# Token mixing of a two-layer trunk: rotation, key stacks, probabilities and values divided anew among VectorE, ScalarE, GpSimd and DMA

## The chip, the cores and the metric

The kernel runs on one core of a Trainium2 chip. The metric is the device time of one execution in microseconds (us). The page and the trace name the engines PE (TensorE's matmuls), PEld (its weight loads), DVE (VectorE), ACT (ScalarE), POOL (GpSimd) and SP (SyncE, which issues the weight loads from HBM). ACTq is ScalarE's queue: DMAs that ScalarE issues are shown there.

## The reference

The reference is a decoder trunk in float32: 256 tokens, width 1024, two layers. Each layer is a half-weighted SwiGLU block, a mixing of tokens, and a second SwiGLU block; a final norm follows. The change lies in the mixing:

```
h = rms_norm(x);  proj = h @ w_in
q, k       = partial rotation of the first 16 of 64 columns of a head:
             (x1*cos - x2*sin, x2*cos + x1*sin, rest)
NSA:  8 query heads, 2 key/value groups; compressed, selected and
      window attention, each times a sigmoid gate, added up
MoBA: 8 heads, causal attention within one block of 256
softmax:  p = exp(s - max) / max(sum, 1);  out = p @ v
x = x + concat(o_nsa, o_moba) @ w_out
```

With 256 tokens all four selected blocks are visible, and the window is wider than the sequence, so the selected and the window attention share scores of plain causal form, one set for each of two key projections.

## The kernel before

The activations are held transposed (features on partitions, tokens along the row). A float32 product is made of three passes in the fp32r format: high part times high part, high times low, low times high. So every weight block of 128x1024 is loaded by SP ("wraw"), cast by ScalarE (line 254, "whi") and subtracted by VectorE (line 283, "wlo"); the class `Stream` hands the blocks to TensorE in the order in which they are used. `pump` and `split` start the splits of blocks to come, as far as the seven slots allow. A scheduler orders each engine's instructions at build time from the order in the source and its own model of durations; at run time each engine's queue is strictly in order.

`mixer` (from line 747) is the mixing of one layer. `feature_one` makes 128 feature rows of a projection in a PSUM bank (four banks "psA", two "psB", one "psC", one "psD"). The rotation of two such sets of rows (128x512 values) is split in two. `rope_begin` (line 759) copies the bank to SBUF ("raw", line 762), has ScalarE issue two DMAs that swap the row pairs to be rotated into SW (lines 763 and 764), and multiplies the bank by the cosine table (line 765, VectorE). `rope_end` (line 767), called later, multiplies SW by the sine table and adds it (lines 768 and 769, both GpSimd). There are seven rotations a layer: query rows 0 and 1, the keys KK, query rows 2 and 3, and four of the MoBA part (`m_feat`, line 1058: keys mk and queries mq, two each; `m_end` ends one).

`stack_q` (line 773) writes a query's high and low part on the two halves of the partitions. `stack_k` (line 798) casts the rotated keys to a high part (line 802, ScalarE) and a low part (line 803, VectorE) on one half of the partitions of KK; `repeat_k` (line 805) copies them to the other half by two DMAs on ScalarE's queue (line 807). `m_stack` and `m_repeat` (lines 1078 to 1093) do the same for the MoBA keys KM.

Scores go to psB and psC (`nsa_s`, line 1026; `moba_s`, line 1188). `softmax` (line 976) masks, scales and takes the maximum on VectorE (lines 984 and 985), then ScalarE exponentiates with a sum (lines 988 and 989). `normalize` (line 992) takes the reciprocals on VectorE and multiplies the probabilities P on GpSimd (lines 1000 and 1001): a 128x256 and a 128x128 part for each of two branches of the eight NSA heads and once for each of the eight MoBA heads. `transpose_p` turns P on TensorE (line 1008) and ScalarE copies it out (line 1010); `pv` multiplies with the values, which ScalarE read from psA with the norm's factor: VN for NSA (line 1122) and MV for MoBA (line 1112, after a `pump` of `m_v`). The output product (`out_block`, lines 539 to 541) takes up the banks of psA afterwards.

Of the kernel before, what the change touches and what calls it, by code (L numbers as in the profile page):

```python
# [21 lines left out]
F32 = mybir.dt.float32  # L22
# [111 lines left out]
def constants():  # L134
# [6 lines left out]
    for h in range(2):  # L141
        for d in range(half):
            C[h * 64 + 8 * d] = C[h * 64 + 8 * d + 4] = cos[:, d]
            Sg[h * 64 + 8 * d] = -sin[:, d]
            Sg[h * 64 + 8 * d + 4] = sin[:, d]
# [165 lines left out]
def trunk(ctx, tc, xin, wst, w1st, gains, glast, cst, small, out, phases=PHASES, n_raw=5, n_hl=7):  # L311
# [435 lines left out]
    def mixer(pi, l):  # L747
# [11 lines left out]
        def rope_begin(b, raw, sw, ro, ctab):  # L759

            src = b.rearrange("p (a t) -> p a t", a=2)
            A.copy(raw, src)
            A.dma_start(sw[0:128:8], raw[4:128:8])
            A.dma_start(sw[4:128:8], raw[0:128:8])
            V.tensor_mul(ro, src, ctab[:, None, :].to_broadcast([128, 2, S]))

        def rope_end(sw, ro, stab):
            G.tensor_mul(sw, sw, stab[:, None, :].to_broadcast([128, 2, S]))
            G.tensor_add(ro, ro, sw)
# [28 lines left out]
        def stack_k():  # L798

            for g in range(2):  # L800
                src = rotk[half[g]].rearrange("p a (b t) -> p b a t", b=2)
                A.copy(KK[g][half[g], 0], src)
                V.tensor_sub(KK[g][half[g], 1], src, KK[g][half[g], 0].bitcast(F32))

        def repeat_k():
            for g in range(2):
                A.dma_start(KK[g][half[1 - g]].bitcast(F32), KK[g][half[g]].bitcast(F32))
# [33 lines left out]
        rotk = rawk[:, 2:4]  # L841
# [5 lines left out]
        rope_begin(b1, rawq[:, 0:2], SW[:, 0:2], rotq[:, 0:2], con("C"))  # L847
# [21 lines left out]
        rope_begin(b2, rawk[:, 0:2], SW[:, 2:4], rotk, CK)  # L869
# [3 lines left out]
        rope_end(SW[:, 0:2], rotq[:, 0:2], con("Sg"))  # L873
# [4 lines left out]
        rope_begin(b3, rawq[:, 2:4], SW[:, 0:2], rotq[:, 2:4], con("C"))  # L878
        rope_end(SW[:, 2:4], rotk, SK)
# [3 lines left out]
        rope_end(SW[:, 0:2], rotq[:, 2:4], con("Sg"))  # L883
        repeat_k()
# [107 lines left out]
        def normalize(key):  # L992
# [6 lines left out]
            for r in range(nb):  # L999
                G.tensor_mul(P[:, 0:2, r], P[:, 0:2, r], sm[:, 0, r:r + 1, None].to_broadcast([128, 2, 128]))  # L1000
                G.tensor_mul(P[:, 2, r], P[:, 2, r], sm[:, 1, r:r + 1].to_broadcast([128, 128]))
# [54 lines left out]
        cur, ends, stacks, reps = {}, [], [], []  # L1056

        def m_feat(which, i):
# [5 lines left out]
            if i % 2 == 1:  # L1064
                h = i // 2
                raw = mp.tile([128, 2, S], F32, name="mraw", tag="F", bufs=2)
                tabs = (CK, SK) if which == "mk" else (con("C"), con("Sg"))
                sw, ro = SW[:, 2 * h:2 * h + 2], cur["rot"][:, 2 * h:2 * h + 2]
                rope_begin(cur["b"], raw, sw, ro, tabs[0])
# [264 lines left out]
```

## Time and profile before

| | us |
|---|---|
| median of 3 runs | 1040.21 |
| lowest, highest run | 1039.88, 1041.37 |
| the profiled execution | 1037.38 |
| its span, first to last instruction | 1035.6 |
| busy: PE, DVE, ACT, POOL | 1000.6, 688.5, 593.3, 326.1 |

The profiled execution is another one than the three timed runs. Its rows are exact for itself alone; a difference of two kernels is read from the timed runs. Busy time of PE counts matmuls that overlap each other, so its share says where PE had nothing under way, not how near it is to its peak. The granted clock of the execution was 0.999 of full speed. The first layer's mixing lies at about 199 to 342 us of the span, the second layer's at about 707 to 851 us.

### The profile page before, as it was taken

Reading aid. Unit: us, or ns where it says so; the run is one execution under the profiler, and the core shown is the slowest. Engines: PE = TensorE matmul, PEld = TensorE weight load, DVE = VectorE, ACT = ScalarE, POOL = GpSimd, SP = SyncE. Lnnn points to the kernel's source line nnn. Section 1 sums busy time; section 2 is a strip of 40 time slices with the busy share of each in tenths; the row PEclk is TensorE's granted clock in tenths of the full one; section 3 lists DMA queues with packets and bytes.
Section 4 is the critical chain, followed back from the end, with each engine's and each line's share of the span. In section 5 each row is a group of like instructions: output and inputs, shape, how many; then the busy total and the mean of one; then the engine's idle time right before and its main releaser. Section 6 shows DMA issues by size and latency. Waiting matters only on the chain.

```text
span 1035.6 us, 16186 instructions
## 1 busy us (share of the span) xinstructions
PE 1000.6 (97%) x5861; PEld 861.0 (83%) x5861; DVE 688.5 (66%) x1187; ACT 593.3 (57%) x1137; POOL 326.1 (31%) x425
## 2 busy tenths in 40 slices
PE   9999999998998999999999999999999989999997
PEld 7788888898776888888888888889888778888885
DVE  6766666589865766566676666566986648666664
ACT  6745555457766655555565555545677747555552
POOL 3622232145641422222232223121475313222230
PEclk9999999999999999999999999999999999999999
DMA  8685776455444466666556677764543426666531
GB/s 268 241 279 186 274 240 218 145 171 157 114 126 125 154 198 196 188 197 186 163 182 203 186 234 239 262 196 138 181 131 108 143 82 208 194 209 193 193 122 41
DMA packets 52848, 188.21 MB, mean 182 GB/s; under 512 B 6368, under 2 KB 6496, under 8 KB 51616
## 3 DMA queue, kind: packets, MB, share of 16 engines
q1 hardware_dynamic: 49680, 182.04, 55.4%
q10 hardware_dynamic: 3088, 5.14, 2.0%
q8 instruction: 46, 0.75, 0.3%
q14 instruction: 34, 0.28, 0.1%
HBM read 182.04 MB, written 1.05 MB: 177 GB/s over the span
## 4 chain that ended last, share of the span: by engine, by line
PE 83%; DVE 7%; ACT 5%; issue 2%; DMA 2%; POOL 1%; ACTq 0%; POOLq 0%; DVEq 0%
PE psB L560 15%; PE psA L539 9%; PE psA L540 9%; PE psA L541 9%; PE psB L562 8%; PE psD L560 8%; PE psC L560 7%; PE psD L562 4%; PE psC L562 4%; DVE wlo L283 3%; PE psA L533 2%; PE psA L532 2%; PE psA L534 2%; ACT whi L254 1%; PE psA L398 1%
## 5 line engine op out<-in xcount | busy, mean ns | idle before, releaser
L283 DVE TENSOR_TENSOR wlo<-wraw,whi 128x1024 fp32r<-128x1024 f32 x325 | 408.2, 1259 | 242.1 <-ACT whi L254 240.5
L254 ACT CAST whi<-wraw 128x1024 fp32r<-128x1024 f32 (+1 forms) x326 | 339.5, 1044 | 304.2 <-issue 175.4
L560 PE MATMUL psB<-x,whi 128*128 128x512 f32 x688 | 243.1, 394 | 3.4 <-DVE hs L627 3.3
L635 POOL TENSOR_TENSOR hs<-hs,rbc 128x256 f32<-128x256 f32 x88 | 75.0, 853 | 380.3 <-DVE hs L627 364.6
L562 PE MATMUL psB<-x,wlo 128*128 128x256 f32 x688 | 192.5, 280 | 0.0
L560 PEld LDWEIGHTS psB<-x,whi 128*128 128x128 f32 x688 | 129.2, 188 | 32.5 <-DVE hs L627 4.3
L541 PE MATMUL psA<-wlo,hp 128*128 128x512 f32 x352 | 136.9, 389 | 0.0
L540 PE MATMUL psA<-whi,hp 128*128 128x512 f32 x352 | 136.8, 389 | 0.0
L539 PE MATMUL psA<-whi,hp 128*128 128x512 f32 x352 | 136.2, 390 | 0.0
L562 PEld LDWEIGHTS psB<-x,wlo 128*128 128x128 f32 x688 | 129.4, 188 | 1.4
L637 POOL TENSOR_TENSOR hs<-hs,rbc 128x256 f32<-128x256 f32 x88 | 102.9, 1170 | 80.5 <-ACT hs L636 80.5
L560 PE MATMUL psC<-x,whi 128*128 128x512 f32 x352 | 124.9, 392 | 0.0
L560 PE MATMUL psD<-x,whi 128*128 128x512 f32 x352 | 124.8, 392 | 0.0
L562 PE MATMUL psC<-x,wlo 128*128 128x256 f32 x352 | 98.6, 280 | 0.9 <-DVE wlo L283 0.9
L562 PE MATMUL psD<-x,wlo 128*128 128x256 f32 x352 | 98.4, 280 | 0.0
L560 PEld LDWEIGHTS psC<-x,whi 128*128 128x128 f32 x352 | 66.1, 188 | 14.5
L560 PEld LDWEIGHTS psD<-x,whi 128*128 128x128 f32 x352 | 66.1, 188 | 14.4
L541 PEld LDWEIGHTS psA<-wlo,hp 128*128 128x128 f32 x352 | 66.1, 188 | 13.9
L539 PEld LDWEIGHTS psA<-whi,hp 128*128 128x128 f32 x352 | 66.0, 188 | 13.7
L540 PEld LDWEIGHTS psA<-whi,hp 128*128 128x128 f32 x352 | 66.1, 188 | 12.3
L532 PE MATMUL psA<-x,whi 128*128 128x256 f32 x256 | 72.8, 284 | 1.2 <-ACT PT L1010 0.8
L533 PE MATMUL psA<-x,whi 128*128 128x256 f32 x256 | 72.3, 283 | 0.7 <-DVE x L380 0.7
(229 smaller groups left out, 1586.3 us busy)
## 6 DMA issues: line engine op xcount, KB each, us to landing
wraw<-in_w SPq DMA_DIRECT2D x318, 512.0 KB, 4.3
W1a<-in_w SPq DMA_DIRECT2D x4, 1024.0 KB, 6.3
W1mixn<-in_w SPq DMA_DIRECT2D x2, 1024.0 KB, 7.6
W1late<-in_w SPq DMA_DIRECT2D x2, 1024.0 KB, 6.5
KM<-KM ACTq DMA_DIRECT2D x8, 256.0 KB, 3.2
wraw<-in_w SPq DMA_DIRECT2D x4, 420.0 KB, 3.7
wraw<-in_w SPq DMA_DIRECT2D x4, 256.0 KB, 5.1
X<-in_small SPq DMA_DIRECT2D x1, 1024.0 KB, 9.5
```

The source lines that it names most:

```text
L254: self.last_hi = self.nc.scalar.copy(hi[:, a:b], raw[:, a:b]).ins
L283: eng.tensor_sub(lo[:, :c], raw[:, :c], hi[:, :c].bitcast(F32))
L532: T.matmul(o, hi, xh, start=first, stop=False, skip_group_check=True)
L533: T.matmul(o, hi, xl, start=False, stop=False, skip_group_check=True)
L534: T.matmul(o, lo, xh, start=False, stop=last, skip_group_check=True)
L539: T.matmul(o, parts[:, 0, c], hi, start=first, stop=False, skip_group_check=True)
L540: T.matmul(o, parts[:, 1, c], hi, start=False, stop=False, skip_group_check=True)
L541: T.matmul(o, parts[:, 0, c], lo, start=False, stop=last, skip_group_check=True)
L560: T.matmul(o, blk128(hi, k), x.rearrange("p a t -> p (a t)"), start=k == 0, stop=k == KT - 1, skip_group_check=True)
L562: T.matmul(o[:, S:], blk128(lo, k), x[:, 0], start=False, stop=k == KT - 1, skip_group_check=True)
L635: G.tensor_mul(g, g, state["rbc"])
L637: G.tensor_mul(g, g, state["rbc5"])
```

## The change

Four parts of the mixing are rewritten, and nothing outside it but the sign of a table.

- Rotation: VectorE multiplies the bank by the sine table (with opposite sign) first, the DMAs swap rows of that product into SW, VectorE multiplies the bank by the cosine table, and `rope_end` is one add on VectorE. The raw copy by ScalarE is made only for the two query sets that the compressed scores read.
- Key stacks: ScalarE and VectorE write both halves of the partitions of KK and KM themselves; `repeat_k` and `m_repeat` with their six DMAs a layer are gone.
- Probabilities: the multiplication by the reciprocal sums is a `tensor_scalar` on VectorE in place of a product on GpSimd.
- Values: of VN and of MV, ScalarE reads the first block of tokens and VectorE the second; MV is read ahead of the `pump` in `m_v(3)` and not after it.

```diff
-            Sg[h * 64 + 8 * d] = -sin[:, d]
-            Sg[h * 64 + 8 * d + 4] = sin[:, d]
+            Sg[h * 64 + 8 * d] = sin[:, d]
+            Sg[h * 64 + 8 * d + 4] = -sin[:, d]
...
-        def rope_begin(b, raw, sw, ro, ctab):
+        def rope_begin(b, raw, other, sw, ro, tabs):
             src = b.rearrange("p (a t) -> p a t", a=2)
-            A.copy(raw, src)
-            A.dma_start(sw[0:128:8], raw[4:128:8])
-            A.dma_start(sw[4:128:8], raw[0:128:8])
-            V.tensor_mul(ro, src, ctab[:, None, :].to_broadcast([128, 2, S]))
-
-        def rope_end(sw, ro, stab):
-            G.tensor_mul(sw, sw, stab[:, None, :].to_broadcast([128, 2, S]))
-            G.tensor_add(ro, ro, sw)
+            ctab, stab = (t[:, None, :].to_broadcast([128, 2, S]) for t in tabs)
+            V.tensor_mul(other, src, stab)
+            A.dma_start(sw[0:128:8], other[4:128:8])
+            A.dma_start(sw[4:128:8], other[0:128:8])
+            V.tensor_mul(ro, src, ctab)
+            if raw is not None:
+                A.copy(raw, src)
+
+        def rope_end(sw, ro):
+            V.tensor_add(ro, ro, sw)
...
-                A.copy(KK[g][half[g], 0], src)
-                V.tensor_sub(KK[g][half[g], 1], src, KK[g][half[g], 0].bitcast(F32))
-
-        def repeat_k():
-            for g in range(2):
-                A.dma_start(KK[g][half[1 - g]].bitcast(F32), KK[g][half[g]].bitcast(F32))
+                own = KK[g][half[g], 0]
+                for r in (half[g], half[1 - g]):
+                    A.copy(KK[g][r, 0], src)
+                for r in (half[g], half[1 - g]):
+                    V.tensor_sub(KK[g][r, 1], src, own.bitcast(F32))
...
-                G.tensor_mul(P[:, 0:2, r], P[:, 0:2, r], sm[:, 0, r:r + 1, None].to_broadcast([128, 2, 128]))
-                G.tensor_mul(P[:, 2, r], P[:, 2, r], sm[:, 1, r:r + 1].to_broadcast([128, 128]))
+                V.tensor_scalar(P[:, 0:2, r], P[:, 0:2, r], sm[:, 0, r:r + 1], None, op0=OP.mult)
+                V.tensor_scalar(P[:, 2, r], P[:, 2, r], sm[:, 1, r:r + 1], None, op0=OP.mult)
...
-                A.copy(K[half[a], :, a, 0], ro[half[a]])
-                V.tensor_sub(K[half[a], :, a, 1], ro[half[a]], K[half[a], :, a, 0].bitcast(F32))
-            reps.append(K)
-
-        def m_repeat():
-            K = reps.pop(0)
-            for a in range(2):
-                A.dma_start(K[half[1 - a], :, a].bitcast(F32), K[half[a], :, a].bitcast(F32))
+                own = K[half[a], :, a, 0]
+                for r in (half[a], half[1 - a]):
+                    A.copy(K[r, :, a, 0], ro[half[a]])
+                for r in (half[a], half[1 - a]):
+                    V.tensor_sub(K[r, :, a, 1], ro[half[a]], own.bitcast(F32))
...
             st.done(u[0])
+            if i == 3:
+                A.activation(MV[:, 0], cur["vb"][0], AF.Copy, scale=rs[:, 0:1])
+                V.tensor_scalar(MV[:, 1], cur["vb"][1], rs[:, 1:2], None, op0=OP.mult)
             st.pump()
-            if i == 3:
-                for blk in range(2):
-                    A.activation(MV[:, blk], cur["vb"][blk], AF.Copy, scale=rs[:, blk:blk + 1])
...
-        for blk in range(2):
-            A.activation(VN[:, blk], vb[blk][:, :S], AF.Copy, scale=rs[:, blk:blk + 1])
+        A.activation(VN[:, 0], vb[0][:, :S], AF.Copy, scale=rs[:, 0:1])
+        V.tensor_scalar(VN[:, 1], vb[1][:, :S], rs[:, 1:2], None, op0=OP.mult)
```

The callers of `rope_begin` and `rope_end` pass both tables, a scratch tile "other" (or, in `m_feat`, a new tile "rots" in place of "mraw"), and no raw tile where none is needed. The calls of `repeat_k` and `m_repeat` are taken out; all other calls keep their order.

## Rows read from the trace of the kernel before

**Rows 1.** The page, part 1: busy us, share of the span, instructions.

```profile
PE 1000.6 (97%) x5861; PEld 861.0 (83%) x5861; DVE 688.5 (66%) x1187; ACT 593.3 (57%) x1137; POOL 326.1 (31%) x425
```

**Rows 2.** Layer 0 in stretches: length, busy (count) of PE, PEld, DVE, ACT, POOL.

```profile
213.00:236.60 23.60, 22.11 (x216) 20.15 (x215) 22.21 (x26) 13.28 (x21) 11.73 (x8) 1.00 0.63 193
236.60:291.00 54.40, 51.41 (x375) 45.17 (x376) 43.04 (x133) 39.16 (x114) 38.34 (x54) 1.00 0.48 138
291.00:332.00 41.00, 36.49 (x206) 27.73 (x205) 25.56 (x71) 26.93 (x65) 9.70 (x14) 1.00 0.42 128
```

**Rows 3.** The waits of PE, 232 to 300 us: total us, times, longest us.

```profile
PE psA L539 <- ACT late L1112: 1.8, 1, 1.8
PE psB L1031 <- DVE qs L778: 1.5, 1, 1.5
PE psD L1048 <- ACT PcT L969: 1.0, 1, 1.0
PE psB L1031 <- DVE mx L984: 1.0, 1, 1.0
...
PE psB L1031 <- DMA KK<-KK: 0.3, 1, 0.3
```

**Rows 4.** The waits of PE, 740 to 810 us (layer 1).

```profile
PE psA L539 <- ACT late L1112: 1.6, 1, 1.6
PE psB L1031 <- DVE qs L778: 1.3, 1, 1.3
```

**Rows 5.** Timeline of ACT's queue: start us, us, what.

```profile
231.18 2.19 ACTq L807 DMA_DIRECT2D KK<-KK  x2
```

**Rows 6.** DMA issues: queue, count, KB each, median us to landing.

```profile
KK<-KK ACTq DMA_DIRECT2D x4, 256.0 KB, 5.3
...
SW<-mraw ACTq DMA_DIRECT2D x16, 32.0 KB, 2.0
```

**Rows 7.** DVE's groups of the whole run: busy us, mean ns, idle before.

```profile
L456 DVE TENSOR_TENSOR yg<-X,gain 128x512 f32<-128x512 f32 x4 | 2.8, 691 | 0.1
...
L465 DVE TENSOR_SCALAR yg<-yg,ny 128x512 f32<-128x512 f32 x2 | 1.0, 486 | 0.1
...
L528 DVE TENSOR_SCALAR gain<-gain 128x1024 f32<-128x1024 f32 x1 | 0.7, 694 | 2.1 <-DMA gain<-in_glast 2.1
```

**Rows 8.** Timeline of DVE: start us, us, instruction, [idle before].

```profile
238.42 1.23 DVE L283 TENSOR_TENSOR wlo<-wraw,whi 128x1024 fp32r<-128x1024 f32 x1 [1.38 <-ACT whi L254]
239.56 0.18 DVE L1119 TENSOR_SCALAR GT<-GT 128x48 f32<-128x48 f32 x1
...
240.15 0.39 DVE L984 CUSTOM_DVE_ANT_0 P<-psB,const,rs 128x256 f32<-128x256 f32 x1
```

**Rows 9.** Line 1001 on POOL: duration ns min/median/max.

```profile
L1001 POOL TENSOR_TENSOR P<-P,sm x48: 389/400/1382, 246.6 to 831.6; 128x128 f32<-128x128 f32 x48
```

**Rows 10.** DVE's groups, 236.6 to 291 us.

```profile
L283 DVE TENSOR_TENSOR wlo<-wraw,whi 128x1024 fp32r<-128x1024 f32 x10 | 13.5, 1351 | 2.8 <-ACT whi L254 2.7
...
L986 DVE TENSOR_SCALAR nm<-mx 128x4 f32<-128x4 f32 x8 | 3.1, 384 | 0.1
L1087 DVE TENSOR_TENSOR KM<-rotmk,KM 64x512 fp32r<-64x512 f32 x2 | 1.9, 972 | 0.0
L1087 DVE TENSOR_TENSOR KM<-rotmq,KM 64x512 fp32r<-64x512 f32 x2 | 1.8, 917 | 2.1 <-ACT KM L1086 2.1
...
L986 DVE TENSOR_SCALAR nm<-mx 128x2 f32<-128x2 f32 x1 | 0.2, 159 | 0.0
```

**Rows 11.** DVE's groups, 213 to 236.6 us.

```profile
L283 DVE TENSOR_TENSOR wlo<-wraw,whi 128x1024 fp32r<-128x1024 f32 x6 | 9.0, 1540 | 0.1
...
L803 DVE TENSOR_TENSOR KK<-rawk,KK 64x512 fp32r<-64x512 f32 x2 | 2.9, 1425 | 0.0
```

**Rows 12.** The waits of DVE and of ACT, 236 to 292 us.

```profile
DVE qs L778 <- ACT qs L776: 3.4, 1, 3.4
...
ACT qs L776 <- POOL rotmq L769: 4.2, 1, 4.2
```

More of the change, by code (lines that the diff above doesn't have):

```diff
@@ L840, in mixer @@
         rawq, rotq, rawk = RW("rawq"), RW("rotq"), RW("rawk")
-        rotk = rawk[:, 2:4]
+        other, rotk = rawk[:, 0:2], rawk[:, 2:4]
         rs = state["rs"]
@@ L846, in mixer @@
         G.tensor_scalar(nrs, rs, -1.0, None, op0=OP.mult)
-        rope_begin(b1, rawq[:, 0:2], SW[:, 0:2], rotq[:, 0:2], con("C"))
+        rope_begin(b1, rawq[:, 0:2], other, SW[:, 0:2], rotq[:, 0:2], (con("C"), con("Sg")))
         st.pump()
@@ L868, in mixer @@
                     V.tensor_mul(Fk[kv][par * 64:(par + 1) * 64, :, g * NC_:(g + 1) * NC_], blocks(src), blocks(rb))
-        rope_begin(b2, rawk[:, 0:2], SW[:, 2:4], rotk, CK)
+        rope_begin(b2, None, other, SW[:, 2:4], rotk, (CK, SK))
         st.pump()
@@ L872, in mixer @@
         feature_one(b3[:, :S], st.use("in", l, 2), True)
-        rope_end(SW[:, 0:2], rotq[:, 0:2], con("Sg"))
+        rope_end(SW[:, 0:2], rotq[:, 0:2])
         for r in (0, 1):
@@ L877, in mixer @@
         feature_one(b3[:, S:], st.use("in", l, 3), False)
-        rope_begin(b3, rawq[:, 2:4], SW[:, 0:2], rotq[:, 2:4], con("C"))
-        rope_end(SW[:, 2:4], rotk, SK)
+        rope_begin(b3, rawq[:, 2:4], other, SW[:, 0:2], rotq[:, 2:4], (con("C"), con("Sg")))
+        rope_end(SW[:, 2:4], rotk)
         stack_k()
@@ L882, in mixer @@
         nsa_v(0)
-        rope_end(SW[:, 0:2], rotq[:, 2:4], con("Sg"))
-        repeat_k()
+        rope_end(SW[:, 0:2], rotq[:, 2:4])
         nsa_v(1)
@@ L1055, in mixer @@
         MV = late[:, 512:1536].rearrange("p (b c) -> p b c", b=2)
-        cur, ends, stacks, reps = {}, [], [], []
+        cur, ends, stacks = {}, [], []
         def m_feat(which, i):
@@ L1065, in m_feat @@
                 h = i // 2
-                raw = mp.tile([128, 2, S], F32, name="mraw", tag="F", bufs=2)
                 tabs = (CK, SK) if which == "mk" else (con("C"), con("Sg"))
                 sw, ro = SW[:, 2 * h:2 * h + 2], cur["rot"][:, 2 * h:2 * h + 2]
-                rope_begin(cur["b"], raw, sw, ro, tabs[0])
-                ends.append((which, h, sw, ro, tabs[1]))
+                rope_begin(cur["b"], None, mp.tile([128, 2, S], F32, name="rots", tag="F", bufs=2), sw, ro, tabs)
+                ends.append((which, h, sw, ro))
             st.pump()
@@ L1075, in m_end @@
             rope_end(*e[2:])
-            stacks.append(e[:2] + e[3:4])
+            stacks.append(e[:2] + e[3:])
         def m_stack():
@@ L1149, in mixer @@
         nsa_s(4)
-        m_repeat()
         nsa_pv(0)
@@ L1217, in mixer @@
         m_end()
-        m_repeat()
         moba_s(0)
```

## The prediction

> **What bounds the kernel now.** I read the page first, for the engines' shares: TensorE is busy 97% of the span and VectorE 66% [rows 1]. So nearly all of the time is matrix work that the change leaves alone, and only TensorE's gaps can be won, or new ones lost. The change touches the mixing stage alone, once a layer, so I went on to the busy times in stretches of the first layer's mixing [rows 2]. The reader is to see two things there. TensorE is idle 1.5, 3.0 and 4.5 us in the three stretches, and VectorE is at 22.2 of 23.6 us in the first, 43.0 of 54.4 in the second, and only 25.6 of 41.0 in the third. The stage is bound by TensorE with VectorE close behind until 291 us, and then by TensorE alone. Last I read the waits of TensorE between 232 and 300 us [rows 3] and for the same work of the second layer [rows 4]: these are the gaps that the change can close.
>
> The wait of 1.5 us for "qs" has a wrong name. Its matmul needs the key stack KK. The two copies of it to the other partitions are issued by ScalarE from 231.18 us on, and such a copy lands 5.3 us after its issue [rows 5, 6], which gives 236.5 us for the first; the next matmul's wait of 0.3 us is named for that copy [rows 3]. I count both waits, 1.8 us in the first layer, and 1.3 in the second, as waits for the copies.
>
> **The change, part by part.** All costs are for one layer, in the middle stretch (236.6 to 291 us) unless I say otherwise.
>
> Rotation. Seven rotations a layer (three in the first stretch, four in the second) lose GpSimd's multiply and add, and get one more VectorE multiply before the swap and a VectorE add after it. Both are 128x512 products or sums; the nearest row is 0.69 us [rows 7]. Four rotations cost 8 x 0.69 = 5.5 us. Five of the seven raw copies leave ScalarE; the two that the compressed scores read stay. The swap's two DMA issues remain on ScalarE's queue, and now wait for VectorE instead of ScalarE's own copy: the splits (the casts of weights) queued behind them can be held. The swap lands in 2.0 us [rows 6], so an add that is reached sooner holds VectorE's queue, softmax included, by 0 to 2.0 us each; that lies within the idle time that the upper bound below keeps.
>
> Key stacks. Six DMA copies and their issues leave ScalarE's queue; it gets six more 64x512 casts, which I cost at nothing, since the issues (two take 2.19 us [rows 5]) go from the same engine; were they to come on top, 4 casts at no more than VectorE's 0.69 us are 2.8 us beside ScalarE's idle 15.2 us in this stretch [rows 2]. VectorE gets four more subtractions of 512 columns here: 4 x 0.69 = 2.8 us [rows 7].
>
> Probabilities. 17 heads' parts are scaled in this stretch (two for each of eight heads, one for the ninth), each by a 128x256 and a 128x128 multiply by a scalar. From 48 columns at 0.18 us [rows 8] to 1024 at 0.69 us [rows 7] is 0.52 ns a column; 512 columns with a scalar read from memory took 0.486 us [rows 7], 0.06 over that line. So I take 0.35 + 0.28 = 0.63 us, and 17 x 0.63 = 10.7 us.
>
> Values. One 128x256 read moves to VectorE, at most the 0.69 us of twice its width [rows 7].
>
> That is 5.5 + 2.8 + 10.7 + 0.7 = 19.7 us in 47 instructions. In the timeline an instruction starts some 0.09 us before the end of the one ahead of it (239.56 against 238.42 + 1.23 [rows 8]), so 47 x 0.09 = 4.2 us overlap, and 15.5 us are added.
>
> Against it stands what VectorE gets back. Where GpSimd reads SBUF at the same time, one holds up the other: GpSimd's 128x128 multiply takes 0.39 us at best and 1.38 at worst [rows 9], and VectorE's rows are longer than the same work undisturbed. In the middle stretch: ten splits 1.351 against 1.23 [rows 8, 10], 1.2 us; eight negations 0.384 against 0.159, 1.8 us; four key subtractions 0.972 and 0.917 against 0.69, 1.0 us [rows 7, 10]. Together 4.0 us, which GpSimd's absence should return.
>
> So VectorE would have 43.0 + 15.5 - 4.0 = 54.5 us of work in a stretch of 54.4 us. In the first stretch the sum is flat: three rotations (6 x 0.60) and two subtractions (2 x 0.60) add 4.8 us, and six splits (1.540 against 1.23) and two key subtractions (1.425 against 0.69 [rows 7, 11]) give back 3.4.
>
> The Trainium skill prices the scaling lower (VectorE: DVE Perf Modes, section on the TRN2 errata): 58 cycles and half a cycle a column in the two-port mode, an estimate of 0.19 + 0.13 us. By that the 17 parts cost 5.4 us and not 10.7, and VectorE would end near 49 us. The row for 48 columns, 0.18 us [rows 8], is twice what the same formula gives, so I keep the rows.
>
> What TensorE gains. (a) The copies' wait: up to 1.8 + 1.3 = 3.1 us over both layers. What is late next is the softmax of the first heads: VectorE reads their scores only at 240.15, after a split that waited 1.38 us for ScalarE [rows 8], and the third pair of score matmuls waits 1.0 us for this bank [rows 3]. I keep half, 1.5 us. (b) The values of the second head group: ScalarE reads both halves with a split between, and the first output block waits 1.8 and 1.6 us [rows 3, 4]. ScalarE comes there late because it stood 4.2 us for the last rotation on GpSimd, and VectorE 3.4 us behind it [rows 12]. With the read ahead of the splits, one half on each engine, a read of 0.69 us remains: 1.1 + 0.9 = 2.0 us won. (c) The wait for PcT (1.0 us [rows 3]) is not touched: nothing.
>
> What VectorE's load costs TensorE. The lower bound is nothing, or a little gain, if the work that slips past 291 us finds the 15.4 idle us of the third stretch [rows 2]. The upper bound: of VectorE's 11.4 idle us in the middle stretch only the 3.4 us behind the last rotation surely go, and if the other 8.0 stay, VectorE ends 8.1 us late in each layer. I take nothing for the forecast, since weight splits, the largest group [rows 10], run ahead of TensorE and can slip, and keep 8.1 for the range.
>
> Sum: 1.5 + 2.0 = 3.5 us less. The profiled execution took 1037.4 us (span 1035.6), 2.8 below the median of 1040.2; 1037.4 - 3.5 = 1033.9, and as a median 1036.7 us.
>
> **The rivals.** Slower, by VectorE's pace: between 236 and 291 us its queue is full and in order, so softmax reads and swapped rows come late, and TensorE waits at the score matmuls. If half of the bound comes true, 2 x 4.05 = 8.1 us are lost; the copies' gain is lost with it, the values' 2.0 us stay: 1040.2 + 6.1 = 1046.3. It decides as soon as VectorE's forced idle time in the middle stretch passes the 1.7 us a layer that are won. For it speaks the sum 54.5 of 54.4; against it that the waits of rows 12 end in GpSimd's chain. The Trainium skill speaks for this rival (Perfetto Trace Analysis, section Optimizing Scalar/DVE Operations): a saturated VectorE should give work away, if need be to GpSimd, though the same place doubts that it helps as both share a port. The trace shows both sides, the full first stretch and the mutual delays.
>
> No change: the copies' wait is simply replaced by the wait for the softmax bank, and the load eats the values' gain; 1040.2 less 0.7 gives 1039.5. For it speaks that VectorE takes up the first scores only at 240.15 [rows 8], 3.7 us after the copy has landed.
>
> Much faster: all the waits of rows 3 and 4 go (5.6 + 2.9 = 8.5 us): 1031.7. Against it: the wait for PcT has no cause in the change.
>
> **How the numbers follow.** Forecast 0.48 (1033 to 1038), much faster 0.08, no change 0.18, slower 0.26. Faster by over 0.2% (2.1 us, what a measurement of this kernel can tell) is 0.56, within it 0.18, slower 0.26. The range goes from a little below the much faster case, 1030, to just beyond the slower one, 1047; what is left out is mostly the full bound of 16 us.
>
> **What would show it.** Right: no wait for KK at the first scores, the wait for the values under 0.8 us, GpSimd nearly empty in the mixing, splits there at 1.23 us, VectorE at 50 to 53 us of the middle stretch and TensorE's gaps in it below 3 us. Wrong: TensorE's waits for VectorE's score reads or for qs grow past 2 us a layer, VectorE waits for SW to land, or splits stay at 1.35 us without GpSimd. Scaling of 128x256 far from 0.35 us would move the sum by 17 times the difference.

## The result, and the profile after

The changed kernel takes 1050.78 us (median of 4 runs, 1049.87 to 1051.18) against 1040.79 for the kernel before on the same chip: a ratio of 1.0098, interval 1.0076 to 1.0119. It is slower by 10 us; the forecast was 1036.7, the range 1030 to 1047, so it lies outside and on the other side of the kernel before.

The page of the changed kernel, part 1, against [rows 1]:

```profile
PE 1008.3 (96%) x5861; PEld 866.7 (83%) x5861; DVE 717.5 (68%) x1327; ACT 595.8 (57%) x1135; POOL 220.7 (21%) x301
```

GpSimd lost 105 us as meant and VectorE gained only 29. TensorE's matmuls are the same 5861, but they are busy for 7.7 us more: some ran slower or overlapped less. The stretches of the first layer [rows 2], then the stretch from the first matmul on "hid" to the transposes of the compressed probabilities (line 968), the part of it from VectorE's read of the compressed scores (line 941) to its last product on them (line 962), and one stretch of 6 us; columns as in [rows 2], with the granted clock, DMA share and GB/s at the end:

```profile
213.00:236.60 23.60, 23.60 (x229) 21.83 (x228) 21.00 (x31) 12.63 (x20) 1.45 (x2) 1.00 0.58 189
236.60:291.00 54.40, 45.94 (x329) 41.36 (x328) 51.90 (x170) 39.91 (x111) 5.71 (x12) 0.91 0.32 101
291.00:332.00 41.00, 40.18 (x231) 31.01 (x230) 30.69 (x99) 26.65 (x65) 0.02 (x1) 1.00 0.42 129
238.87:273.98 35.11, 27.20 (x201) 24.53 (x199) 33.61 (x109) 23.89 (x66) 5.39 (x10) 0.90 0.36 111
...
257.19:273.44 16.25, 11.17 (x86) 9.28 (x85) 16.12 (x53) 10.64 (x32) 1.87 (x3) 0.91 0.33 102
...
268.00:274.00 6.00, 0.44 (x4) 0.24 (x2) 5.93 (x20) 3.53 (x11) 1.31 (x2) 0.70 0.36 100
```

The same two stretches of the kernel before (its lines 940 to 961):

```profile
237.39:261.87 24.48, 22.96 (x184) 21.23 (x182) 22.40 (x70) 18.20 (x52) 16.55 (x23) 1.00 0.52 157
...
251.34:261.30 9.96, 9.96 (x84) 9.26 (x82) 9.62 (x29) 8.17 (x22) 8.73 (x11) 1.00 0.55 148
```

The three stretches of 213 to 332 us are the same times in both kernels and not quite the same work, since the changed kernel enters the mixing 2.1 us later. In the first and the last of them TensorE's gaps are gone: none before 236.6 us (1.5 us before), and 0.8 in place of 4.5 us after 291. The loss is between, where its gaps are 8.5 us and not 3.0. From "hid" to the compressed transposes it took 24.5 us and takes 35.1, and VectorE is busy 96% of that (92% before). In it, between reading the compressed scores and finishing their probabilities VectorE has 53 instructions and not 29, and is full to 0.13 us; TensorE has 11.2 us of other work, and then stands. The weight splits of VectorE between "hid" and those transposes, first before, then changed:

```profile
L283 DVE TENSOR_TENSOR wlo<-wraw,whi 128x1024 fp32r<-128x1024 f32 x5 | 6.7, 1342 | 1.4 <-ACT whi L254 1.4
```

```profile
L283 DVE TENSOR_TENSOR wlo<-wraw,whi 128x1024 fp32r<-128x1024 f32 x8 | 9.8, 1220 | 0.6 <-ACT whi L254 0.6
```

Three more of them stand ahead of the product, beside what the change itself adds. The waits of TensorE between 232 and 300 us, against [rows 3]:

```profile
PE psA L968 <- DVE Pc L962: 5.6, 1, 5.6
PE psB L1032 <- DVE mx L985: 1.5, 1, 1.5
PE psA L921 <- POOL gh L909: 0.7, 1, 0.7
PE psC L1034 <- ACT hid L890: 0.6, 1, 0.6
```

The waits for "qs", KK, PcT and late are gone, and one of 5.6 us (5.3 in the second layer) has taken their place; the wait for the compressed product was 0.3 us before. VectorE's groups between 236.6 and 291 us, against [rows 10]:

```profile
L283 DVE TENSOR_TENSOR wlo<-wraw,whi 128x1024 fp32r<-128x1024 f32 x10 | 12.2, 1219 | 0.6 <-ACT whi L254 0.6
...
L1001 DVE TENSOR_SCALAR P<-P,sm 128x256 f32<-128x256 f32 x14 | 4.9, 347 | 0.1
L1002 DVE TENSOR_SCALAR P<-P,sm 128x128 f32<-128x128 f32 x14 | 3.9, 279 | 0.0
...
L1090 DVE TENSOR_TENSOR KM<-rotmk,KM 64x512 fp32r<-64x512 f32 x4 | 2.7, 685 | 0.1
L764 DVE TENSOR_TENSOR rots<-psA,const 128x512 f32<-128x512 f32 x2 | 1.4, 684 | 0.0
...
L987 DVE TENSOR_SCALAR nm<-mx 128x4 f32<-128x4 f32 x8 | 1.3, 165 | 0.0
```

Every price and the relief came as forecast; the loss does not come from a wrong price of an instruction.

**How the time divides.** For each layer I took the mixing from the first transposes of X (line 398) to the broadcast of the next norm (line 514) and subtracted the gaps between TensorE's rows of the timeline; what is left is "rest". "Half" is how long, by windows of 0.5 us, TensorE worked at a granted clock of half (1.2 GHz in place of 2.4).

| us, layer 0 / 1 | mixing | gaps | rest | half |
|---|---|---|---|---|
| before | 148.3 / 148.8 | 9.5 / 9.5 | 138.8 / 139.2 | 0 / 0 |
| changed | 153.6 / 154.0 | 11.4 / 12.0 | 142.2 / 142.0 | 6.7 / 5.5 |

So a layer loses 5.3 us, twice that is the 10 us. Standing grew by 1.9 to 2.5 us only, since the new stand of 5.6 us came in the place of the waits that went. The other 2.8 to 3.4 us lie in the rest, with the half clock. In the first layer only half of the 6.7 us of work at half clock lies behind the stand, in a stretch that begins while TensorE stands (0.70 granted from 268 to 274 us above); the other half comes 18 us ahead of it, at 246.5 to 250.0 us, where TensorE never stands:

```profile
247.00:250.00 3.00, 3.00 (x16) 3.00 (x16) 3.00 (x11) 1.80 (x8) 0.00 (x0) 0.51 0.53 193
```

This division holds for two single executions. They differ by more than the medians (1050.5 against 1037.4): the first transposes of X come at 195.7 and not 193.6 us, though nothing up to there is changed. A row of the changed kernel shows a reason, beside that of the kernel before:

```profile
35.00:38.00 3.00, 3.00 (x11) 2.52 (x10) 1.02 (x2) 2.33 (x4) 3.00 (x4) 0.50 0.88 305
```

```profile
35.00:38.00 3.00, 3.00 (x19) 2.66 (x18) 0.61 (x3) 2.92 (x6) 3.00 (x5) 1.00 0.81 294
```

And the profiled execution of the kernel before had nearly no half clock (0.999 granted on average), while its other executions on record were granted 0.994 in the median, and those of the changed kernel 0.989 to 0.990. By these averages a usual execution of the changed kernel has some 10 us more at half clock than a usual one of the kernel before, and not 21 as the two profiles have. At the 0.47 us for each that the section on the clock finds, an estimate of at most 4.5 of the 10 us is the clock's, for part of that time TensorE stands; the standing of the table, 4.4 us in both layers, is most of the rest.

### The profile page after: what moved, and what is told of

It is laid out like the page before. It is cut to its first block, busy times and chain, and to the rows that moved or that the text cites. A ratio compares the mean times of both kernels' runs of the same rounds, so it can differ in the third digit from the quotient of the medians.

```text
span 1048.7 us, 16112 instructions
## 1 busy us (share of the span) xinstructions
PE 1008.3 (96%) x5861; PEld 866.7 (83%) x5861; DVE 717.5 (68%) x1327; ACT 595.8 (57%) x1135; POOL 220.7 (21%) x301
## 4 chain that ended last, share of the span: by engine, by line
PE 84%; DVE 9%; issue 3%; ACT 2%; DMA 1%; POOL 1%; ACTq 0%; DVEq 0%
PE psB L560 15%; PE psA L540 9%; PE psA L541 9%; PE psA L539 9%; PE psD L560 8%; PE psB L562 7%; PE psC L560 7%; PE psD L562 4%; PE psC L562 4%; DVE wlo L283 3%; PE psA L533 1%; PE psA L532 1%; PE psA L534 1%; PE psA L1009 1%; PE psD L1018 1%
## 5 line engine op out<-in xcount | busy, mean ns | idle before, releaser
L283 DVE TENSOR_TENSOR wlo<-wraw,whi 128x1024 fp32r<-128x1024 f32 x325 | 400.0, 1233 | 242.4 <-ACT whi L254 241.0
L532 PE MATMUL psA<-x,whi 128*128 128x256 f32 x256 | 74.1, 290 | 0.4 <-DVE X L409 0.4
L533 PE MATMUL psA<-x,whi 128*128 128x256 f32 x256 | 73.5, 287 | 0.7 <-DVE x L380 0.7
```

Source lines behind the costliest of these rows:

```text
L283: eng.tensor_sub(lo[:, :c], raw[:, :c], hi[:, :c].bitcast(F32))
L532: T.matmul(o, hi, xh, start=first, stop=False, skip_group_check=True)
L533: T.matmul(o, hi, xl, start=False, stop=False, skip_group_check=True)
```

## Experiments

Two theories stood at first. **Load**: VectorE is full, so what it is given delays what TensorE waits for. **Order**: the compressed probabilities merely stand too late in a queue. Behind each expectation stand the median, the ratio to the kernel before in the same runs, and the ratio's 95% interval.

**Single parts and pairs**, each from the kernel before with the named parts of the change's diff:

Scaling alone.

```diff
-                G.tensor_mul(P[:, 0:2, r], P[:, 0:2, r], sm[:, 0, r:r + 1, None].to_broadcast([128, 2, 128]))
...
+                V.tensor_scalar(P[:, 0:2, r], P[:, 0:2, r], sm[:, 0, r:r + 1], None, op0=OP.mult)
...
```

> The kernel before with one part of the change alone: the probabilities are scaled on VectorE. Load theory: VectorE has some 43 + 8 us of work in the 54 us stretch, less 2 to 3 us that GpSimd no longer disturbs, so it nearly fits: Pc waited for by 0 to 2 us a layer, 1039 to 1045 us. Order theory: no wait of over 1 us, 1040 us. If the scaling alone were the whole loss: 1049 us or more.

1043.15 us, ratio 1.0032 (1.0021 to 1.0042): slower, with waits of 2.2 and 3.4 us at the compressed transposes (first and second layer).

Rotation alone (`rope_begin`, `rope_end` and their callers as in the change).

> The kernel before with the new rotation alone (VectorE multiplies first, rows of the product are swapped, VectorE adds). Load theory: 5 us more for VectorE in the stretch, 1 to 2 us less disturbance, 1037 to 1042 us. Rotation theory: VectorE stands for the swapped rows, 1 us or more in each of seven rotations, and the time is 1046 us or more.

1039.12, 0.9991 (0.9977 to 1.0005): no difference; GpSimd is relieved, but KK's copies are waited for longer (8.9 us in both layers).

Key stacks and values together (without rotation and scaling).

> The kernel before with the two other parts alone: key stacks written on both halves without DMA, and half of the values read by VectorE ahead of the split. Load theory: VectorE gets some 3.5 us a layer in the stretch, which fits; the wait for KK (1.8 and 1.3 us) and most of the wait for the values (1.8 and 1.6) go: 1035 to 1039 us. If the gains are given back at the next wait: 1040 us.

1034.40, 0.9947 (0.9927 to 0.9967): **faster than both kernels**. The part between the compressed scores and their product, and the longest wait of TensorE for this work in both layers, in this kernel (called the good pair from here on):

```profile
250.80:258.58 7.78, 7.78 (x65) 7.55 (x64) 6.63 (x25) 5.40 (x19) 6.77 (x11) 1.00 0.22 67
```

```profile
PE psB L1029 <- DVE mx L982: 8.2, 4, 2.6
```

VectorE has 25 instructions there, TensorE works through, and what is waited for more than before is the maxima of the first scores.

Key stacks alone, and values alone.

```diff
...
-            A.activation(VN[:, blk], vb[blk][:, :S], AF.Copy, scale=rs[:, blk:blk + 1])
+        A.activation(VN[:, 0], vb[0][:, :S], AF.Copy, scale=rs[:, 0:1])
+        V.tensor_scalar(VN[:, 1], vb[1][:, :S], rs[:, 1:2], None, op0=OP.mult)
```

> The kernel before with the key stacks alone written directly (both halves cast by ScalarE and subtracted by VectorE, no DMA copies). By the prediction's terms the wait for the copies of KK goes (1.5 to 3.1 us a layer) and VectorE takes 2.8 us a layer more beside other work: 1034 to 1038. The rest of the 5.4 us that key stacks and values gained together is then the values' (0 to 4 us). Rival (VectorE's added subtractions lengthen the queue between compressed scores and their product): 1040 to 1043, with a wait at the two transposes.

> The kernel before with the values alone changed: half of the scaled values (one 128x256 and one 128x512 read of a bank a layer) by VectorE and not ScalarE. By the prediction's term (b) the waits of TensorE for late (3.4 us in two layers) and the like go: 1036 to 1039. If keys alone (1041.4) and values alone added, key stacks and values together (1034.4) would leave 1033 for this run. Rival (it only pays together with the key stacks, through the order of VectorE's queue): 1039 to 1042.

Keys 1041.39, 1.0013 (1.0003 to 1.0024); values 1037.33, 0.9970 (0.9958 to 0.9982). Apart they make +0.13% and -0.30%, together -0.53%; the intervals of the values alone and of the pair overlap, so whether the keys add to the values is not sure. Keys alone came out where the rival had it, but not by the rival's wait: at the two transposes TensorE waits 0.5 and 1.0 us. The wait for the copies is gone (1.8 and 1.3 us; the "1.5 to 3.1 us a layer" of the expectation took the sum of both layers for one), but TensorE waits 3.7 us for maxima in the first layer and works 6.2 to 6.4 us a layer at half clock.

The changed kernel with the scaling given back to GpSimd (run a second time for its profile, since the execution that was profiled first took 2010.8 us; why is not known), and with the rotation undone:

```diff
-                V.tensor_scalar(P[:, 0:2, r], P[:, 0:2, r], sm[:, 0, r:r + 1], None, op0=OP.mult)
...
+                G.tensor_mul(P[:, 0:2, r], P[:, 0:2, r], sm[:, 0, r:r + 1, None].to_broadcast([128, 2, 128]))
...
```

> The changed kernel with one part undone: the probabilities are multiplied on GpSimd again. Load theory (VectorE has more work than the stretch from 236 to 291 us holds): 10 of the 15 us that were added per layer go, the wait of TensorE for the compressed probabilities Pc falls from 5.5 us a layer to under 1, and the time is 1034 to 1041 us. Order theory (the turn of Pc stands too early in TensorE's queue, whatever VectorE's load): the wait stays over 3 us a layer and the time at 1046 or more. Rotation theory (the wait for the swapped rows in VectorE's queue): the time stays over 1046, and VectorE waits for SW.

> The same kernel as in e1_scale_pool, for a profile that can be read. Its time of 1046.1 us was 5 us over what the load theory allowed. Order theory: TensorE still stands 3 us or more a layer for the compressed probabilities Pc or for the read of the scores, although VectorE is under 50 of 54 us busy between 236 and 291 us. Rotation theory: VectorE's queue stands for the swapped rows SW. Load theory, what is left of it: VectorE is over 52 us busy there, by more than my rows gave.

> The changed kernel with the rotation alone undone: key stacks, values and scaling on VectorE stay. If the parts simply add up, scaling +3.3 and keys with values -5.4 give 1037.7 us. Load theory: VectorE has 5 us less than in the changed kernel, 49 to 51 of 54 us, and TensorE stands for Pc 0 to 3 us a layer: 1036 to 1043 us. If it is the number of steps that the compressed probabilities queue behind, and not the rotation, it stays at 1047 or more.

1046.09, 1.0055 (1.0034 to 1.0075), and 1048.56 in the one execution of the second time; without rotation 1052.21, 1.0112 (1.0096 to 1.0128). The parts do not add. Rotation on the good pair costs 11.7 us, scaling on it 17.8; alone, by the kernel before in the same runs (1039.82), they cost -0.7 and +3.3. Undoing the scaling leaves over half of the loss, undoing the rotation all of it. Both times lie outside what load theory allowed (1034 to 1041 and 1036 to 1043): taking an engine's microseconds off a stage is not enough to say what comes back.

**Is it the order?** Two runs on the changed kernel. VectorE's queue with the compressed chain first:

```diff
         c_scores()
-        normalize(2)
...
+        with tc.issue_after(cmp_["first"]):
+            normalize(2)
...
         c_normalize()
-        normalize(3)
...
+        with tc.issue_after(cmp_["last"]):
+            normalize(3)
```

> The changed kernel with another order on VectorE alone: behind the maximum of the compressed scores, and behind the product that normalizes them, stand the pieces of rotation, key stacks, splits and probabilities that got ahead of them; no work is added or taken away. Order theory: the 5.5 us that TensorE stands for Pc in each layer fall under 1.5, and the time to 1037 to 1043 us. Load theory: VectorE has the same work, so what Pc no longer waits for is waited for elsewhere: 1047 to 1053 us.

And the compressed transposes later on TensorE, behind the next feature block:

```diff
-        c_transpose()
         nsa_s(4)
+        m_feat("mk", 3)
+        c_transpose()
...
-        m_feat("mk", 3)
```

> The changed kernel with another order on TensorE: a feature block of 2.8 us is put ahead of the turn of the compressed probabilities. Order theory: TensorE's stand for Pc shrinks by 2.8 us a layer or goes, 1042 to 1046 us, and the clock no longer falls behind it. Load theory: the wait moves to the next piece that needs VectorE, 1048 to 1052 us.

1049.52, 1.0084 (1.0064 to 1.0104), and 1052.60, 1.0119 (1.0104 to 1.0134). With the chain first the waits of TensorE read

```profile
PE psB L1032 <- DVE mx L985: 9.4, 4, 3.2
PE psA L1009 <- DVE P L1002: 3.7, 2, 2.0
```

The wait moved from the compressed product to the maxima and to P, all of them VectorE's, and the gaps of a layer stayed (11.2 and 11.6 us). With the transposes later the wait was 6.5 us in each layer, longer and not shorter. The simple order theory falls.

**Is it VectorE's time?** The good pair (keys and values), plus dead multiplications on VectorE that nobody reads, queued behind the reciprocal sums ("own" below), GpSimd scaling P as before:

```diff
...
+                with tc.issue_after(own):
+                    V.tensor_scalar(dum[:, :256], dum[:, :256], 0.5, None, op0=OP.mult)
+                    V.tensor_scalar(dum[:, 256:], dum[:, 256:], 0.5, None, op0=OP.mult)
```

> Key stacks and values as changed, rotation and the scaling of P as before, and beside GpSimd's scaling VectorE runs the same two multiplications on a scratch tile that nobody reads, queued behind the reciprocal sums: VectorE gets the load of the scaling without anything depending on it. Key stacks and values alone took 1034.4, with the scaling really on VectorE 1052.2. Load theory (what costs is the VectorE time that stands in the queue, whatever it computes): 1046 to 1056, the two transposes of the compressed probabilities wait for VectorE again, and VectorE is over 94% busy from the hidden rows of the compression to those transposes. Rival (what costs is that P is now finished by VectorE, late in its queue): 1034 to 1040.

1052.40, 1.0123 (1.0106 to 1.0140): the dead load alone makes the faster kernel as slow as the change. At a mean of 0.44 and 0.35 us, beside GpSimd at work, it is a quarter heavier than the scaling of the change. The part between the compressed scores and product, and the wait for it in both layers:

```profile
258.54:274.42 15.88, 10.87 (x86) 9.32 (x84) 15.82 (x45) 12.16 (x31) 11.64 (x15) 0.92 0.19 61
```

```profile
PE psA L967 <- DVE Pc L961: 9.8, 2, 5.0
```

The same with 128x16 in place of 128x256 and 128x128:

> As e11_load (key stacks and values as changed; dead multiplications on VectorE behind the reciprocal sums), but the dead multiplications are 128x16 and not 128x256 and 128x128: the same number of instructions in nearly the same places of VectorE's queue, at perhaps 0.1 to 0.2 us each in place of 0.44 and 0.35. VectorE's queue between the compressed scores and their product has 42 rows (e11: 40, key stacks and values alone: 22). Load theory: the time falls to 1034 to 1041, with at most 2 us of waiting at the two transposes in each layer. Order theory (the rows between count): it stays at 1046 to 1054.

1049.18, 1.0086 (1.0062 to 1.0109): far outside load theory's 1034 to 1041. It tells less than meant, since VectorE stayed as full: 33.4 us of work from "hid" to the compressed transposes, and 33.8 with the wide ones. A thin instruction took 0.17 us in the median, but some took up to 1.2 us, so the means are 0.31 and 0.27 us; and the queue of this kernel has one split more between the compressed scores and their product.

The weight splits that `m_feat` starts given to GpSimd, all or every second:

```diff
-            st.pump()
+            st.pump(pool=True)
```

> The changed kernel with the weight splits that the feature blocks of the MoBA part start (m_feat) subtracted by GpSimd and not by VectorE: some 8 of the 10 splits of the middle stretch, 1.2 us each, so about 10 us a layer off VectorE, onto a GpSimd that is busy 5 of 35 us there. A split on GpSimd should take 2.5 to 4 us by the 1.3 to 1.9 us of its 128x512 operations. Load theory: the wait of 5.6 and 5.3 us at the two transposes falls under 2 us, VectorE falls to about 80% between the hidden rows and those transposes, and the time is 1030 to 1042. Rival (the queue's order or the clock decides, not VectorE's time; or TensorE now waits for splits that GpSimd makes late): 1045 to 1060, with waits at the weights.

> As e13, but only every second feature block gives its splits to GpSimd: about 5 us a layer off VectorE. Load theory: between the changed kernel (1050.8) and e13, 1038 to 1046, with 1 to 4 us of waiting at the two transposes in each layer. Rival (order or clock decides): no such order; it may lie outside these two.

1057.25, 1.0169 (1.0145 to 1.0192), and 1061.12, 1.0201 (1.0181 to 1.0221): far off what load theory expected for the time. The waits at the compressed transposes did go (none, and 0.4 us a layer), but TensorE waits elsewhere and its gaps are 13.0 to 15.2 us a layer. The groups of VectorE in the first of them, from "hid" to the compressed transposes, and the timelines of GpSimd and VectorE around 241 us, show why:

```profile
L1001 DVE TENSOR_SCALAR P<-P,sm 128x256 f32<-128x256 f32 x8 | 6.5, 814 | 0.1
...
L1116 DVE TENSOR_SCALAR GT<-GT 128x48 f32<-128x48 f32 x1 | 2.3, 2282 | 0.8 <-ACT GT L1115 0.8
```

```profile
240.83 4.68 POOL L283 TENSOR_TENSOR wlo<-wraw,whi 128x1024 fp32r<-128x1024 f32 x2 [22.96 <-ACT whi L254]
```

```profile
240.97 2.28 DVE L1116 TENSOR_SCALAR GT<-GT 128x48 f32<-128x48 f32 x1 [0.75 <-ACT GT L1115]
```

A 128x48 addition took 2.28 us beside a split of 2.4 us on GpSimd, where it took 0.18 us before [rows 8]. VectorE was not relieved: it stayed 88% busy there. So these two runs do not decide about load theory. The Trainium skill (Trainium Architecture — The Big Picture, section "What this means for kernel authors") calls the port pair that the two engines share an exclusive lock and not a split of bandwidth; the row agrees.

Last, the load taken away with nothing put in its place: the changed kernel without the scaling, and with one block in two scaled (both leave out work that the reference has).

```diff
             for r in range(nb):
-                V.tensor_scalar(P[:, 0:2, r], P[:, 0:2, r], sm[:, 0, r:r + 1], None, op0=OP.mult)
-                V.tensor_scalar(P[:, 2, r], P[:, 2, r], sm[:, 1, r:r + 1], None, op0=OP.mult)
```

> The changed kernel without the multiplication of P by its inverse sums (left out on every engine: the mixing adds unnormalised probabilities); rotation, key stacks and values as changed, GpSimd as idle as in the changed kernel. This takes about 0.63 us for each of 24 multiplication pairs a layer, 17 of them in the middle stretch, off VectorE. VectorE's queue between the compressed scores and their product has 40 rows (changed kernel 50, before 25), so its order is still the new one. Load theory: from the hidden rows to the two transposes VectorE has some 28 us to do and not 33.6, that stretch takes 29 to 31 us and not 35, the wait at the transposes falls to 0 to 3 us, and the time is 1034 to 1043. Rival (the order of the queue or the clock decides): 1045 to 1051.

> As e17, but the first of the two blocks of P in each head is multiplied by VectorE, the others are left out: half of the load. Load theory: between e17 and the changed kernel, 1041 to 1048, with 2 to 5 us of wait at the two transposes in each layer. Rival: within 2 us of either.

1041.15, 1.0000 (0.9984 to 1.0016), and 1050.09, 1.0093 (1.0076 to 1.0110). Without scaling the wait is 2.4 us, and 9.6 us come back. In its profile the clock does not fall in the mixing; that profile is of the fastest of its ten executions (1037.2 us), and the others were granted 0.988 to 0.998. Half the scaling gave nothing back, against the expected middle. The two parts between compressed scores and product, first without, then with half the scaling:

```profile
254.28:267.64 13.36, 10.47 (x82) 8.65 (x80) 13.18 (x43) 11.73 (x36) 0.62 (x1) 1.00 0.35 118
```

```profile
257.20:273.34 16.14, 10.32 (x85) 9.09 (x83) 15.89 (x49) 10.49 (x32) 0.97 (x3) 0.90 0.32 107
```

With half the scaling, VectorE's queue is as long there as in the changed kernel (16.14 against 16.25 us): 1.2 us of scaling are gone, the same three weight splits stand in it, and one more add of a rotation (0.7 us). The scheduler makes the queue anew for each kernel and fills part of what is freed.

That gives one rule for the wait at this place. In each kernel with a wait of over 2 us there, VectorE is 98 to 99.7% busy between reading the compressed scores and finishing their probabilities, and TensorE stands for what this takes beyond its own work in that time (layer 0, us; the first three columns from windows as above). The difference is bookkeeping, queue less work; what the windows show is that VectorE is full meanwhile, so the queue's length is its work:

| kernel | VectorE's queue, instructions | TensorE's work | difference | wait named |
|---|---|---|---|---|
| values alone | 7.8, 25 | 7.8 | 0 | none |
| keys and values | 7.8, 25 | 7.8 | 0 | none |
| rotation alone | 9.3, 34 | 9.3 | 0 | none |
| before | 10.0, 29 | 10.0 | 0 | 0.3 |
| splits on GpSimd | 7.1, 28 | 7.1 | 0 | none |
| every second split on GpSimd | 10.9, 36 | 10.2 | 0.7 | 0.4 |
| chain first | 11.0, 39 | 11.0 | 0 | none |
| keys alone | 12.7, 37 | 12.7 | 0 | 0.5 |
| scaling on GpSimd again | 13.2, 40 | 10.6 | 2.6 | 2.8 |
| no scaling | 13.4, 43 | 10.5 | 2.9 | 2.4 |
| scaling alone | 13.5, 44 | 9.9 | 3.6 | 2.2 and 0.7 |
| dead load | 15.9, 45 | 10.9 | 5.0 | 5.0 |
| half the scaling | 16.1, 49 | 10.3 | 5.8 | 6.4 |
| changed | 16.3, 53 | 11.2 | 5.1 | 5.6 |
| transposes later | 16.9, 53 | 10.9 | 6.0 | 6.5 |
| thin dead load | 17.4, 47 | 12.5 | 4.8 | 5.5 |
| rotation undone | 19.0, 54 | 12.6 | 6.4 | 7.8 |

The rule gives one wait and not the time: the chain first (1049.5 us) and the splits on GpSimd (1057.3) are slow without a wait here.

**Is the clock a cost of its own?** A pair on the changed kernel: the compressed transposes pinned ahead of all that follows them in the source but the next scores (`nsa_s(4)`); and the same with 48 matmuls of zeros ahead of them.

```diff
...
+            with tc.issue_after(cmp_["s4"]):
+                for _ in range(48):
+                    T.matmul(b[:, :256], zero[:, :128], zero, start=True, stop=True)
             for blk in range(2):
-                T.transpose(b[:, blk * 128:(blk + 1) * 128], P[:, blk].rearrange("p h n -> p (h n)"), ident)
+                turn = T.transpose(b[:, blk * 128:(blk + 1) * 128], P[:, blk].rearrange("p h n -> p (h n)"), ident)
...
```

> The changed kernel with the order on TensorE pinned: the two transposes of the compressed probabilities go ahead of everything that follows them in the source (about 30 rows earlier in TensorE's queue), nothing is left out. It is the pair of the run with filler matmuls. Queue theory (VectorE's queue between the compressed scores and their normalised product is too long; TensorE stands at these transposes until it is done): the product comes when it comes, so TensorE stands longer there, 7 to 10 us a layer instead of 5.6 and 5.3, and the time is 1050 to 1056. Rival (the order on TensorE decides): the time moves below 1047 or above 1060.

> As the run before it, with 48 matmuls of zeros (128x256 bf16) put into TensorE's queue just ahead of the two transposes, into the bank that the transposes then overwrite: about 5.7 us of work a layer in place of standing, if each takes 0.118 us. Clock theory (after the stand TensorE runs for a while at half the clock, and that is a second cost of about a third of the time spent there): the stretch at 1.2 GHz behind the transposes is gone, the time that TensorE is neither standing nor filling falls by 2 to 4 us a layer, and the run is 3 to 8 us faster than its pair. Rival (a half clock costs nothing, since VectorE sets the pace): the run is within 1 us of its pair, or slower.

1057.14, 1.0165 (1.0141 to 1.0190), with waits of 9.0 and 9.2 us, as the queue rule expects (the time is 1 us over its bound); and 1057.91, 1.0175 (1.0154 to 1.0196): no gain. The fillers ran (5.4 us a layer), the wait fell to 4.0, but the half clock did not go away (10.2 us in the first layer's mixing with and without them). Windows of the second:

```profile
244.00:251.00 7.00, 7.00 (x33) 7.00 (x34) 6.29 (x23) 3.79 (x17) 0.74 (x2) 0.53 0.51 138
271.00:275.00 4.00, 4.00 (x24) 2.59 (x25) 1.85 (x9) 0.42 (x2) 0.00 (x0) 0.57 0.02 4
```

TensorE worked through both stretches at little over half the clock. So the run cannot price the clock by taking it away. What does is the run with the chain first, where both layers have the same instructions in the same order. Its windows from "hid" to the compressed transposes, layer 0 and 1:

```profile
238.59:268.59 30.00, 27.70 (x201) 25.98 (x200) 26.86 (x96) 21.03 (x60) 4.46 (x8) 0.89 0.25 75
754.85:782.42 27.57, 25.10 (x201) 23.11 (x199) 26.69 (x97) 21.05 (x60) 4.46 (x8) 1.00 0.26 83
```

The same 201 matmuls take 2.6 us longer at a granted 0.89. Over the whole mixing, layer 0 worked 13.5 us at half clock and layer 1 4.9; with gaps of 11.2 and 11.6 us the mixing took 155.9 and 152.6. Over the 38 layers of the 19 usable profiles, the rest (mixing less gaps, less fillers) rises by 0.47 us for each microsecond of work at half clock (correlation 0.92), from 138.5 us without any. So the price of the half clock is measured; that the load causes it is not shown for all of it.

## Why the prediction was wrong

- **Prices and relief: right.** Scaling 0.347 and 0.279 us against 0.35 and 0.28; rotation 0.684 against 0.69. Relief: splits 1.22 us, negations 0.165, key subtractions 0.685; ten, eight and four of them make 1.3 + 1.8 + 1.0 = 4.1 us against the 4.0 forecast. VectorE has 51.9 us in the middle stretch and not 54.5, as three of the 17 scalings slid behind 291 us, where it has 5.1 us more. The lower figures that the prediction took for the scaling from the Trainium skill (VectorE: DVE Perf Modes, section on the TRN2 errata), by estimate 0.19 and 0.13 us, are not borne out. The same section says that its row comes out too low and that the measured fixed term is about 150 cycles and not 58; that gives by estimate 0.29 and 0.22 us, and the dead multiplications by a constant took 0.288 and 0.222 us in the median.
- **Gain (a): right that the wait goes; that half stays won is not borne out.** The first stretch has no gap left, but the next wait, for the first maxima, took it up, as the text warned: keys alone are 1.5 us slower.
- **Gain (b): right.** 2.0 us forecast, 3.5 by the values alone (1.9 to 4.4 by the interval).
- **The step that failed: "What VectorE's load costs TensorE ... I take nothing for the forecast, since weight splits ... run ahead of TensorE and can slip", and with it (c), the wait for PcT "is not touched: nothing".** No row showed a split slipping, and the upper bound of 8.1 us a layer was kept for the range alone. The sum of 54.5 in 54.4 us was a mean over a stretch whose first 24.5 us, up to the compressed transposes, were already 92% full (22.40 of 24.48). There the queue got 11.2 us more (33.61), while the slack counted on lay behind the transposes. And splits could not slip: an in-order queue whose order is fixed at build time holds them, eight and not five, ahead of the compressed product. TensorE's own queue is in order too, so it stood 5.6 and 5.3 us for that one late product.
- **A term that was missing.** The sum moved TensorE's gaps only. TensorE also worked at half clock, 5.5 to 6.7 us a layer in the profile, which made 2.8 to 3.4 us a layer there and by the estimate above up to 4.5 us for both layers together in usual executions. The rival "slower, by VectorE's pace" (1046.3) falls short of the measured 1050.8 by just that much, which is in part luck, since half of its bound was a guess. That rival had the mechanism; it named the score matmuls as the place, and its price stopped at the stand. Its half of the bound, 4.05 us a layer, lies under the measured 5.3.
- **The signs were poorly chosen.** Of the six signs of being right five came: no wait for KK, none for the values, GpSimd nearly empty, splits at 1.22 us, VectorE at 51.9 us. Only TensorE's gaps in the middle stretch, 8.5 us and not below 3, told the truth. Of the signs of being wrong the first did not come: the wait for the score reads is 1.5 and 1.6 us, that for qs is gone, and what grew was the wait for another of VectorE's products. VectorE did wait for SW to land, which was the second sign:

```profile
DVE rotq L772 <- DMA SW<-rawk: 4.9, 2, 2.6
```

That is both layers' wait for the second rotation. In the first layer it lies ahead of 236.6 us, where TensorE has no gap, so the loss does not come from it, though 2.6 us is over the 2.0 that the prediction allowed for one.

- **A reading that was short.** The "much faster" case sums the waits of [rows 4], which leave out others of the second layer (for PcT and for the maxima 1.0 us each, three shorter ones); with these its 1031.7 us would be lower. It decided nothing.
- **The skill's doubt held for one kind of work and not for another.** The Trainium skill (Perfetto Trace Analysis, section Optimizing Scalar/DVE Operations) says that it may make sense to take work off a saturated VectorE, and doubts that GpSimd is a place for it. Leaving the scaling out gave 9.6 us; giving it to GpSimd gave 4.7 (1046.1 against 1050.8), while the weight splits on GpSimd cost 6 to 10 us more.

Open: what makes the clock fall at 246.5 us, behind stands of 1.5 and 0.7 us (the kernel without scaling has the same two stands and no fall), and why matmuls of zeros did not hold it up. So it stays open how much of the half clock is the load's doing. The clock's share of the medians is an estimate only: executions of the kernel before range from 1036.7 to 1042.8 us, and the only one profiled (1037.4) had no half clock in the mixing. Open too is what the amount of work does by itself and what the order, which the scheduler makes anew for every kernel: a version with the good pair and a pinned order on every engine was not tried.

## What to carry to other kernels

Add up an engine's work not over a stage but up to each result that another engine's in-order queue will stop for; slack that lies behind that result does not help it. Here that stretch was 92% full, and 11.2 us more in it came out as a stand of 5.6 us. When a change makes TensorE stand, look at the granted clock of the matrix work behind the stand as well. And take a change apart before judging it: two of its four parts made the kernel 0.5% faster, and the four together 1% slower.

## What the runs showed of the hardware that was not expected

In the first layer's mixing of the changed kernel the granted clock was 0.5 for 10 us in all: 3.4 us of work at 246.5 us, and 6.8 us during and behind the stand of 5.6 us. Behind a stand of 2.2 us (scaling alone, first layer) it fell too; behind the ones of 2.4 us without scaling it stayed at 1.00. An execution has half clock in code that the change does not touch as well (at 35 us in the changed kernel's profile, not in that of the kernel before). A small VectorE instruction can take nearly the whole length of one of GpSimd's (2.28 us beside a split of 2.4, in place of 0.18). A multiplication of 128x16 on VectorE, by a constant and in place, took 0.17 us in the median and up to 1.2 us with GpSimd at work; one of 128x256 took 0.29 in the median and up to 1.4.
